# Four of twenty-two inner tiles of each feed-forward leave the seven-product scheme on their way out

## The chip, the cores and the metric

The kernel runs on one core of a Trainium2 chip. TensorE (PE) multiplies, VectorE (DVE), ScalarE (ACT) and GpSimd (POOL) do the elementwise work, SyncE (SP) issues the DMAs. Each engine works through its own queue in order, and semaphores tie the queues together. The metric is the device time of one launch in microseconds, the median of repeated runs; beside it stands one profiled launch, from which every row below is taken.

## The reference

One block of a decoder: a feed-forward, a token mixer (pooling and a gated delta rule), and a second feed-forward, each behind an RMS norm with shift and scale and a gate from a conditioning vector. Only the two feed-forwards are touched by the change:

```python
def swiglu(h, w_in, w_out):
    gate, up = jnp.split(h @ w_in, 2, axis=-1)
    return (jax.nn.silu(gate) * up) @ w_out

x = x + 0.5 * gate[:, 0, None, :] * swiglu(h, ffn1_w_in[l], ffn1_w_out[l])
```

There are 1024 tokens, the model width is 1024 and the hidden width 2816, which is 22 inner tiles of 128. All is float32.

## The kernel before

**Data.** Activations lie with the model dimension on partitions: `x[k][hf]` is 128 rows of the width by one half (512) of the tokens, k from 0 to 7, hf 0 or 1. A float32 operand is split into a high part, which ACT casts to the type fp32r (L134), and a low part, which DVE subtracts (L135). A product of two split operands takes three matmuls of 128x128 by 512. Weights come by DMA into `raw` (seven buffers), and their split halves go to `whi`/`wlo` (a ring of three pairs in the feed-forwards).

**In.** For an inner tile f, `both` forms gate and up for both halves of the tokens. It does so by a seven-product scheme of the Strassen-Winograd kind: seven `product` calls of 12 matmuls (L440, 84 in all), with DVE sums of weights and of PSUM banks between them, and a `yield` behind each product. At its end `gated_tile` (L457) multiplies silu(gate) by up and leaves the two halves as plain float32 tiles `gf`. The pool "g" has N_G = 10 buffers.

**Out.** Tiles 0 and 1 go plainly: `sweep` runs them through `middle` (plain products), splits the results (`gated`), and `out` calls `accumulate` (L297 to L304): for each 128 rows of the output six matmuls and one DVE update of x (L303). Tiles 2 to 21 go in five groups of four through `out_group`: seven products n = 1, 6, 7, 2, 4, 5, 3, each over two pairs of tiles (p = 0, 1), 12 matmuls a piece, 168 a group, a `yield` behind each of the 14 steps. Each step splits a weight and a tile (`oph`/`opl`); n = 6, 2 and 5 also form sums and differences (eight a pair, sixteen a group); when p = 1, DVE updates x from the banks (L555), 32 updates a group.

**Order.** `ffn` weaves them: while the `both` steps of a group run, every second one is followed by one step of the group before. So the 28 steps in of one group carry the 14 steps out of the group before. Behind the last group nothing is left to weave with: its 14 steps run alone, with their sums on POOL (`eng=G`, lines L371, L525, L538) in place of DVE. x of half 0 is complete when n = 4 has been added; at n = 5 `done(0)` begins what follows for half 0, while the 48 matmuls of n = 5 and 3 still run for half 1. In the first feed-forward `done(0)` is the norm in front of the mixer (`squares`, `rstd_rows`, `norm_steps`: L230 to L273); in the second it is the final norm and the store (`finish`, L751 to L771). The framework's planner lays down each engine's queue from the order in which the code emits the instructions and from its own forecast of when each is ready.

PSUM has eight banks; out products use `PSUM_OUT = ("inv", "inv", "scan", "oo")`, in products `pj` and `t`, two each.

Of the kernel before, what the change touches and what calls it, by code (L numbers as in the profile page):

```python
# [13 lines left out]
ALU = mybir.AluOpType  # L14
AX = mybir.AxisListType

P = 128
# [3 lines left out]
HALF = 512  # L21
# [45 lines left out]
def block(tc, ctx, xT, vec, cst, invw, ada_w, f1_in, f1_out, f2_in, f2_out, mix_in, mix_ba,  # L67
# [229 lines left out]
    def accumulate(x, gs, ws, gate, hf, mh, steps):  # L297

        for m in range(NC):
# [4 lines left out]
                                   in1=x[k][hf], op0=ALU.mult, op1=ALU.add)  # L304
            next(steps, None)

    def sweep(n, ins, outs, middle, x, gate, done=None, lead=None, between=iter(())):


        for j in range(0, n, 2):  # L310
            js = (j, j + 1)
            last = j == n - 2
            g = {}

            def middles(pairs):
                w = {}
                for i, hf in pairs:
                    if i not in w:
                        w[i] = ins(i)
                    g[i, hf] = middle(i, hf, w[i])  # L320

            def out(hfs, steps=iter(())):
                for mh in range(NH):
                    ws = [outs(i, mh) for i in js]
                    for hf in hfs:
                        accumulate(x, [g[i, hf] for i in js], ws, gate, hf, mh, steps)
                for _ in steps:
                    pass

            if lead:  # L330
                out(range(NH), lead(js, middles, g))
            elif last:
                steps = None
                for hf in range(NH):
                    middles([(i, hf) for i in js])
                    out([hf], steps or iter(()))
                    steps = done(hf)
            else:
                middles([(i, hf) for i in js for hf in range(NH)] if j else
                        [(i, hf) for hf in range(NH) for i in js])  # L340
                out(range(NH), islice(between, 5 * NC))
# [7 lines left out]
    def ffn(fpool, x, h, w_in, w_out, gate, done, between=(), first=None):  # L349
# [20 lines left out]
        def sub(out, a, b, eng=V):  # L370
            eng.tensor_tensor(out=out, in0=a, in1=b, op=ALU.subtract)  # L371
# [75 lines left out]
            for k in range(4):  # L447
                terms(ps, w, hs[k], k, start and k == 0, k == 3, not start)

        def both(f, out):  # L450

            (a11, a12), (a21, a22) = [[load(w_in[f, :, i, c * HALF:(c + 1) * HALF])
                                       for c in range(2)] for i in range(2)]
            h11, h21, h22 = h[0][:4], h[0][4:], h[1][4:]
            s1, s2 = nt[:, 0, :], nt[:, 1, :]

            def gated_tile(a, b):  # L457
                t = fpool.tile([P, HALF], F32, tag="g", name="gf", bufs=N_G)
                V.tensor_tensor(out=t, in0=a, in1=b, op=ALU.mult)
                out.append(t)  # L460

            c11, c12 = bank("pj"), bank("t")
            product(c11, a11, h11)
            yield
            u = act()
            S.copy(u, c11)
            V.tensor_tensor(out=s1, in0=a21, in1=a22, op=ALU.add)
            product(c12, s1, sums["1"])
            yield
            v = act()  # L470
            S.copy(v, c12)
            sub(s2, s1, a11)
            product(c11, a12, h21, start=False)
            yield
            g0 = act()
            S.activation(g0, c11, AF.Silu)
            p6 = bank("pj")
            product(p6, s2, sums["2"])
            yield
            V.tensor_tensor(out=u, in0=u, in1=p6, op=ALU.add)  # L480
            sub(s2, a12, s2)
            product(c12, s2, h22, start=False)
            yield
            g1 = act()
            V.tensor_tensor(out=g1, in0=u, in1=c12, op=ALU.add)
            S.activation(g1, g1, AF.Silu)
            p7 = bank("t")
            sub(s1, a11, a21)
            product(p7, s1, sums["3"])
            yield  # L490
            V.tensor_tensor(out=u, in0=u, in1=p7, op=ALU.add)
            V.tensor_tensor(out=v, in0=u, in1=v, op=ALU.add)
            p4 = bank("pj")
            product(p4, a22, sums["4"])
            yield
            V.tensor_tensor(out=u, in0=u, in1=p4, op=ALU.subtract)
            gated_tile(g0, u)
            gated_tile(g1, v)

        def out_group(fs, gs, eng=V, half_done=None):  # L500


            def w(f, mh):
                return load(w_out[f * P:(f + 1) * P, mh * HALF:(mh + 1) * HALF])

            def s_tile():
                return fpool.tile([P, HALF], F32, tag="s", name="s", bufs=2)

            ab = [(fs[i], fs[i + 1], gs[fs[i]], gs[fs[i + 1]]) for i in range(0, GROUP, 2)]
            s2, s3 = {}, {}  # L510
            banks, steps = None, iter(())
            for n in (1, 6, 7, 2, 4, 5, 3):
                if n in (1, 2, 4, 5):
                    banks = [bank(tag) for tag in PSUM_OUT]
                chained = n in (6, 7, 3)
                if n == 5 and half_done:
                    steps = half_done()
                for p, (f0, f1, (b11, b12), (b21, b22)) in enumerate(ab):

                    if n == 1:  # L520
                        a, b = w(f0, 0), b11
                    elif n == 6:
                        a11, a21, a22 = w(f0, 0), w(f0, 1), w(f1, 1)
                        sub(b12, b22, b12, eng)
                        eng.tensor_tensor(out=b11, in0=b11, in1=b12, op=ALU.add)  # L525
                        s2[p], s3[p] = s_tile(), a11
                        sub(a11, a11, a21, eng)
                        sub(s2[p], a22, a11, eng)
                        a, b = s2[p], b11
                    elif n == 7:  # L530
                        a, b = s3[p], b12
                    elif n == 2:
                        a, b = w(f1, 0), b21
                    elif n == 4:
                        a, b = w(f1, 1), b21
                    elif n == 5:
                        a, a22, b = w(f0, 1), w(f1, 1), b11
                        eng.tensor_tensor(out=a, in0=a, in1=a22, op=ALU.add)  # L538
                    else:
                        a, b = s2[p], b22  # L540
                    ah, op = pair(), tuple(fpool.tile([P, HALF], F32R, tag="op" + e, name="op" + e,
                                                      bufs=N_OP) for e in "hl")
                    split(a, *ah)
                    split(b, *op)
                    if n == 2:
                        sub(s2[p], a, s2[p], eng)
                        sub(b21, b21, b11, eng)
                        sub(b11, b22, b11, eng)
                    for m in range(NC):
                        terms(banks[m], ah, op, m, p == 0 and not chained, p == 1, chained)  # L550
                        if p == 1:
                            for mh, hf in {1: [(0, 0)], 6: [(0, 1)], 7: [(1, 0), (1, 1)], 2: [(0, 0)],
                                           4: [(1, 0)], 5: [(1, 1)], 3: [(0, 1)]}[n]:
                                k = mh * NC + m
                                V.scalar_tensor_tensor(out=x[k][hf], in0=banks[m],  # L555
                                                       scalar=mod[:, gate, k:k + 1], in1=x[k][hf],
                                                       op0=ALU.mult, op1=ALU.add)
                        next(steps, None)
                    yield
            for _ in steps:  # L560
                pass

        pools = ExitStack()
        steps = chain(h_sums(), between)
        sweep(2, lambda f: [weight(w_in[f, :, i, :], D) for i in range(2)],
              lambda f, mh: weight(w_out[f * P:(f + 1) * P, mh * HALF:(mh + 1) * HALF], HALF)[0],
              middle, x, gate, lead=lead)
        outs = iter(())
        for f0 in range(2, FT, GROUP):
            fs = list(range(f0, f0 + GROUP))  # L570
            gs = {f: [] for f in fs}
            for i, _ in enumerate(chain(*(both(f, gs[f]) for f in fs))):
                next(steps, None)
                if i % 2:
                    next(outs, None)
            last = f0 + GROUP == FT
            outs = out_group(fs, gs, G if last else V, (lambda: done(0)) if last else None)
        for _ in steps:
            pass
        for _ in outs:  # L580
            pass
        done(1)
        pools.close()

# [834 lines left out]
```

## Time and profile before

| what | value |
|---|---|
| median of 3 runs | 2564.01 us (2563.77 to 2565.46) |
| profiled launch, its own time | 2562.3 us |
| span of its instructions | 2560.5 us |
| mean granted TensorE clock, as a share | 0.982 |
| PE busy / weight loads busy / DVE / ACT / POOL | 96% / 79% / 76% / 39% / 10% |

The first feed-forward ends near 750 us, the mixer runs from there, and the second feed-forward fills the end from near 1890 us. A matmul's listed time (0.39 us) is longer than the distance between two starts, because matmuls overlap; so PE's pace is read from starts, or from counts in a window.

### The profile page before, as it was taken

Reading aid. Unit: us, or ns where it says so; the run is one execution under the profiler, and the core shown is the slowest. Engines: PE = TensorE matmul, PEld = TensorE weight load, DVE = VectorE, ACT = ScalarE, POOL = GpSimd, SP = SyncE. Lnnn points to the kernel's source line nnn. Section 1 sums busy time; section 2 is a strip of 40 time slices with the busy share of each in tenths; the row PEclk is TensorE's granted clock in tenths of the full one; section 3 lists DMA queues with packets and bytes.
Section 4 is the critical chain, followed back from the end, with each engine's and each line's share of the span. In section 5 each row is a group of like instructions: output and inputs, shape, how many; then the busy total and the mean of one; then the engine's idle time right before and its main releaser. Section 6 shows DMA issues by size and latency. Waiting matters only on the chain. (4 is left out here: it accounts for less than half of the span.)

```text
span 2560.5 us, 33699 instructions
## 1 busy us (share of the span) xinstructions
PE 2460.6 (96%) x12472; PEld 2015.4 (79%) x12472; DVE 1954.1 (76%) x3320; ACT 1010.8 (39%) x1710; POOL 267.1 (10%) x266
## 2 busy tenths in 40 slices
PE   5899999999979999999999999999999999999996
PEld 5678888888757888888888888788777888888874
DVE  5998978888767867767778853677678687888887
ACT  3433333333345544454454542311453333333333
POOL 2400000000240001012000000000250000000024
PEclk9999999999989999999999999999999999999997
DMA  7334422222221121121111122754321222222221
GB/s 231 110 114 125 140 79 73 69 67 80 95 107 55 34 66 64 47 72 62 47 46 46 38 88 91 250 190 152 91 66 50 64 82 69 70 70 66 80 88 68
DMA packets 122710, 224.21 MB, mean 88 GB/s; under 512 B 13744, under 2 KB 14512, under 8 KB 122544
## 3 DMA queue, kind: packets, MB, share of 16 engines
q1 hardware_dynamic: 122544, 222.04, 27.1%
q8 instruction: 98, 1.61, 0.2%
q14 instruction: 68, 0.56, 0.1%
HBM read 196.82 MB, written 25.17 MB: 87 GB/s over the span
## 5 line engine op out<-in xcount | busy, mean ns | idle before, releaser
L134 ACT CAST whi<-raw 128x512 fp32r<-128x512 f32 (+1 forms) x403 | 247.9, 617 | 608.3 <-PE ps_pj L165 157.4
L135 DVE TENSOR_TENSOR wlo<-raw,whi 128x512 fp32r<-128x512 f32 (+1 forms) x403 | 287.5, 717 | 87.2 <-ACT whi L134 85.6
L165 PE MATMUL ps_pj<-hh,whi 128*128 128x512 f32 (+1 forms) x732 | 304.6, 416 | 4.2 <-ACT whi L134 4.2
L165 PE MATMUL ps_pj<-hl,whi 128*128 128x512 f32 (+1 forms) x732 | 289.7, 396 | 0.0
L165 PE MATMUL ps_pj<-hh,wlo 128*128 128x512 f32 (+1 forms) x732 | 289.7, 396 | 0.0
L134 ACT CAST whi<-nt 128x512 fp32r<-128x512 f32 x160 | 99.3, 621 | 238.2 <-PE ps_pj L440 131.9
L165 PEld LDWEIGHTS ps_pj<-hh,whi 128*128 128x128 f32 (+1 forms) x732 | 137.6, 188 | 28.8 <-ACT whi L134 4.6
L165 PEld LDWEIGHTS ps_pj<-hh,wlo 128*128 128x128 f32 (+1 forms) x732 | 137.1, 187 | 28.8 <-issue 0.2
L165 PEld LDWEIGHTS ps_pj<-hl,whi 128*128 128x128 f32 (+1 forms) x732 | 137.8, 188 | 23.0 <-issue 1.2
L135 DVE TENSOR_TENSOR wlo<-nt,whi 128x512 fp32r<-128x512 f32 x160 | 112.0, 701 | 50.9 <-ACT whi L134 50.0
L440 PE MATMUL ps_pj<-hh,wlo 128*128 128x512 f32 x320 | 124.8, 390 | 1.0 <-DVE wlo L135 1.0
L440 PE MATMUL ps_pj<-hh,whi 128*128 128x512 f32 x320 | 124.9, 390 | 0.0
L440 PE MATMUL ps_pj<-hl,whi 128*128 128x512 f32 x320 | 124.8, 390 | 0.0
L371 POOL TENSOR_TENSOR gf<-gf 128x512 f32<-128x512 f32 x12 | 20.9, 1746 | 991.5 <-ACT whi L134 965.1
L440 PE MATMUL ps_inv<-opl,whi 128*128 128x512 f32 x280 | 113.2, 404 | 4.9 <-DVE opl L135 4.4
L440 PE MATMUL ps_inv<-oph,whi 128*128 128x512 f32 x280 | 110.5, 398 | 5.7 <-DVE x L555 4.4
L555 DVE SCALAR_TENSOR_TENSOR x<-ps_inv,mod,x 128x512 f32<-128x512 f32 x160 | 111.7, 743 | 2.7 <-PE ps_inv L440 2.5
L440 PE MATMUL ps_inv<-oph,wlo 128*128 128x512 f32 x280 | 111.3, 398 | 0.0
L135 DVE TENSOR_TENSOR opl<-gf,oph 128x512 fp32r<-128x512 f32 x140 | 103.0, 739 | 6.6 <-ACT oph L134 6.2
L862 DVE SCALAR_TENSOR_TENSOR cacc<-rawseq,vt,cacc 128x512 f32<-128x512 f32 x144 | 107.3, 746 | 0.6
L165 PE MATMUL ps_pj<-hxh,whi 128*128 128x512 f32 (+1 forms) x252 | 103.3, 411 | 0.0
L134 ACT CAST oph<-gf 128x512 fp32r<-128x512 f32 x140 | 86.3, 616 | 36.5 <-PE ps_oo L440 26.6
(465 smaller groups left out, 6404.1 us busy)
## 6 DMA issues: line engine op xcount, KB each, us to landing
raw<-f_in SPq DMA_DIRECT2D x184, 256.0 KB, 3.4
raw<-f_out SPq DMA_DIRECT2D x168, 256.0 KB, 2.8
raw<-ada_w SPq DMA_DIRECT2D x112, 256.0 KB, 3.1
raw<-mix_in SPq DMA_DIRECT2D x104, 256.0 KB, 2.8
ada_raw<-ada_w SPq DMA_DIRECT2D x32, 256.0 KB, 3.7
sg_dram<-sg SPq DMA_DIRECT2D x32, 256.0 KB, 2.0
act<-sg_dram SPq DMA_DIRECT2D x32, 256.0 KB, 4.1
raw<-dn_proj SPq DMA_DIRECT2D x20, 256.0 KB, 2.9
```

Source lines behind the costliest of these rows:

```text
L134: S.copy(hi, src)
L135: lo_eng.tensor_tensor(out=lo, in0=src, in1=hi.bitcast(F32), op=ALU.subtract)
L165: PE.matmul(ps, lhsT=a, rhs=b, start=n == 0, stop=n == last)
L371: eng.tensor_tensor(out=out, in0=a, in1=b, op=ALU.subtract)
L440: PE.matmul(ps, lhsT=u[:, c * P:(c + 1) * P], rhs=v, start=start and n == 0, stop=stop and n == 2, skip_group_check=chained)
L555: V.scalar_tensor_tensor(out=x[k][hf], in0=banks[m], scalar=mod[:, gate, k:k + 1], in1=x[k][hf], op0=ALU.mult, op1=ALU.add)
L862: V.scalar_tensor_tensor(out=acc, in0=raw[:, i:i + HALF], scalar=w[:, i:i + 1], in1=acc, op0=ALU.mult, op1=ALU.add)
```

## The change

Tiles 2 and 3 are formed by `both` as before, but leave as split pairs (`pairs=True`), and a new function `out_pair` runs them plainly through `accumulate`, half 1 first. Four groups of four (tiles 4 to 19) stay. Tiles 20 and 21 are formed by `both` as split pairs too; one step of the last group follows every one of their 14 steps (`each=1`). Then `out_pair` runs tiles 20 and 21 plainly, first half 0 alone, then half 1 alone with the steps of `done(0)` between its products; the weights are loaded and split for each of the two calls. `out_group` loses its engine choice (all its sums are on DVE) and its call of `done(0)`.

```diff
+    def out_pair(outs, js, g, hfs, x, gate, steps=iter(())):
+        for mh in range(NH):
+            ws = [outs(i, mh) for i in js]
+            for hf in hfs:
+                accumulate(x, [g[i, hf] for i in js], ws, gate, hf, mh, steps)
+        for _ in steps:
+            pass
...
             def gated_tile(a, b):
+                if pairs:
+                    V.tensor_tensor(out=a, in0=a, in1=b, op=ALU.mult)
+                    out.append(gated(fpool, a))
+                    return
...
-        def out_group(fs, gs, eng=V, half_done=None):
+        def out_group(fs, gs):
...
-                if n == 5 and half_done:
-                    steps = half_done()
...
+        def tiles_of(fs, outs, each, pairs=False):
+            gs = {f: [] for f in fs}
+            for i, _ in enumerate(chain(*(both(f, gs[f], pairs) for f in fs))):
+                next(steps, None)
+                if i % each == each - 1:
+                    next(outs, None)
+            for _ in outs:
+                pass
+            return {(f, hf): gs[f][hf] for f in fs for hf in range(NH)} if pairs else gs
+
         outs = iter(())
-        for f0 in range(2, FT, GROUP):
+        js = (2, 3)
+        out_pair(pair_out, js, tiles_of(js, outs, 2, True), (1, 0), x, gate)
+        for f0 in range(4, FT - 2, GROUP):
             fs = list(range(f0, f0 + GROUP))
-            gs = {f: [] for f in fs}
-            for i, _ in enumerate(chain(*(both(f, gs[f]) for f in fs))):
-                next(steps, None)
-                if i % 2:
-                    next(outs, None)
-            last = f0 + GROUP == FT
-            outs = out_group(fs, gs, G if last else V, (lambda: done(0)) if last else None)
+            outs = out_group(fs, tiles_of(fs, outs, 2))
+        js = (FT - 2, FT - 1)
+        g = tiles_of(js, outs, 1, True)
         for _ in steps:
             pass
-        for _ in outs:
-            pass
+        out_pair(pair_out, js, g, [0], x, gate)
+        out_pair(pair_out, js, g, [1], x, gate, done(0))
         done(1)
```

## Rows read from the trace of the kernel before

**Rows 1.** The page: busy time, then PE's busy tenths in 40 slices.

```profile
PE 2460.6 (96%) x12472; PEld 2015.4 (79%) x12472; DVE 1954.1 (76%) x3320; ACT 1010.8 (39%) x1710; POOL 267.1 (10%) x266
PE   5899999999979999999999999999999999999996
```

**Rows 2.** Busy by window, second feed-forward: two tiles unwoven, then one woven group.

```profile
core 0: us, PE busy (x) PEld busy (x) DVE busy (x) ACT busy (x) POOL busy (x), PEclk, DMA share, GB/s
1982.00:2020.70 38.70, 38.70 (x169) 31.55 (x168) 25.18 (x40) 13.54 (x23) 0.00 (x0) 1.00 0.19 57
...
2251.70:2367.20 115.50, 115.50 (x506) 94.62 (x505) 93.81 (x150) 41.80 (x72) 0.00 (x0) 1.00 0.24 73
```

**Rows 3.** First feed-forward's end in order of time: start, length, what.

```profile
689.46 0.62 PE L440 MATMUL ps_inv<-oph,whi 128*128 128x512 f32 x2
...
724.64 0.39 PE L440 MATMUL ps_oo<-oph,wlo 128*128 128x512 f32 x1
...
725.53 0.74 DVE L555 SCALAR_TENSOR_TENSOR x<-ps_oo,mod,x 128x512 f32<-128x512 f32 x1
...
749.41 0.40 PE L440 MATMUL ps_oo<-oph,wlo 128*128 128x512 f32 x1
...
753.97 0.69 PE L165 MATMUL ps_pj<-hh,whi 128*64 128x512 f32 x1 [4.16 <-ACT whi L134]
```

**Rows 4.** Second feed-forward's end in order of time.

```profile
2483.49 0.62 PE L440 MATMUL ps_inv<-oph,whi 128*128 128x512 f32 x2
...
2518.95 0.39 PE L440 MATMUL ps_oo<-oph,wlo 128*128 128x512 f32 x1
...
2519.38 0.75 DVE L555 SCALAR_TENSOR_TENSOR x<-ps_oo,mod,x 128x512 f32<-128x512 f32 x1
...
2537.41 0.39 PE L440 MATMUL ps_oo<-oph,wlo 128*128 128x512 f32 x1
...
2545.72 0.69 DVE L230 TENSOR_TENSOR act<-act,nt 128x512 f32<-128x512 f32 x1
...
2551.78 5.36 DVE L770 SCALAR_TENSOR_TENSOR x<-x,vt,ps_pj 128x512 f32<-128x512 f32 x8 [3.25 <-PE ps_pj L175]
```

**Rows 5.** What PE waited for, 688.7 to 770 us: total, times, longest.

```profile
PE ps_scan L440 <- DVE x L555: 2.6, 5, 1.3
PE ps_oo L440 <- DVE x L555: 2.4, 5, 1.1
```

**Rows 6.** Plain out products at the mixer's end, in order of time.

```profile
1721.05 0.39 PE L165 MATMUL ps_inv<-gh,whi 128*128 128x512 f32 x1
...
1721.73 0.39 PE L165 MATMUL ps_inv<-gh,whi 128*128 128x512 f32 x1
```

**Rows 7.** DVE's two commonest forms in 2251.7 to 2367.2 us: busy, mean ns.

```profile
L135 DVE TENSOR_TENSOR wlo<-raw,whi 128x512 fp32r<-128x512 f32 x22 | 15.1, 687 | 4.1 <-ACT whi L134 3.9
...
L555 DVE SCALAR_TENSOR_TENSOR x<-ps_inv,mod,x 128x512 f32<-128x512 f32 x16 | 11.1, 743 | 0.0
```

**Rows 8.** The page's DMA issues: the weights of the way out.

```profile
raw<-f_out SPq DMA_DIRECT2D x168, 256.0 KB, 2.8
```

**Rows 9.** PE in `sweep` of tiles 0 and 1, second feed-forward, weight change.

```profile
1929.23 0.50 PE L165 MATMUL ps_inv<-gh,whi 128*128 128x512 f32 x1 [0.92 <-DVE x L303]
1931.09 0.50 PE L165 MATMUL ps_inv<-gh,wlo 128*128 128x512 f32 x1 [1.13 <-DVE wlo L135]
```

**Rows 10.** The norm of half 0 and the mixer's first weights, first feed-forward.

```profile
735.98 2.72 DVE L268 SCALAR_TENSOR_TENSOR nt<-x,coef,ps_pj 128x512 f32<-128x512 f32 x4 [0.74 <-PE ps_pj L175]
...
740.85 9.18 POOL L135 TENSOR_TENSOR hl<-nt,hh 128x512 fp32r<-128x512 f32 x7 [0.45 <-ACT hh L134]
...
753.31 2.17 ACT L134 CAST whi<-raw 128x512 fp32r<-128x512 f32 x4
```

**Rows 11.** `finish` of half 0, and the sums of squares of half 1.

```profile
2527.12 1.06 PE L247 MATMUL ps_t<-ct,act 128*128 128x1 f32 x8
...
2531.39 11.75 POOL L768 TENSOR_TENSOR x<-x,act 128x512 f32<-128x512 f32 x8 [1.91 <-ACT act L762]
...
2538.65 6.24 DVE L230 TENSOR_TENSOR act<-act,nt 128x512 f32<-128x512 f32 x5
```

More of the change, by code (lines that the diff above doesn't have):

```diff
@@ L322, in out @@
             def out(hfs, steps=iter(())):
[L323 to L327, printed above, removed]
-                    pass
+                out_pair(outs, js, g, hfs, x, gate, steps)
             if lead:
@@ L448, in product, with both @@
                 terms(ps, w, hs[k], k, start and k == 0, k == 3, not start)
-        def both(f, out):
+        def both(f, out, pairs=False):
             (a11, a12), (a21, a22) = [[load(w_in[f, :, i, c * HALF:(c + 1) * HALF])
@@ L510, in out_group @@
             s2, s3 = {}, {}
-            banks, steps = None, iter(())
+            banks = None
             for n in (1, 6, 7, 2, 4, 5, 3):
@@ L523, in out_group @@
                         a11, a21, a22 = w(f0, 0), w(f0, 1), w(f1, 1)
-                        sub(b12, b22, b12, eng)
-                        eng.tensor_tensor(out=b11, in0=b11, in1=b12, op=ALU.add)
+                        sub(b12, b22, b12)
+                        V.tensor_tensor(out=b11, in0=b11, in1=b12, op=ALU.add)
                         s2[p], s3[p] = s_tile(), a11
-                        sub(a11, a11, a21, eng)
-                        sub(s2[p], a22, a11, eng)
+                        sub(a11, a11, a21)
+                        sub(s2[p], a22, a11)
                         a, b = s2[p], b11
@@ L537, in out_group @@
                         a, a22, b = w(f0, 1), w(f1, 1), b11
-                        eng.tensor_tensor(out=a, in0=a, in1=a22, op=ALU.add)
+                        V.tensor_tensor(out=a, in0=a, in1=a22, op=ALU.add)
                     else:
@@ L545, in out_group @@
                     if n == 2:
-                        sub(s2[p], a, s2[p], eng)
-                        sub(b21, b21, b11, eng)
-                        sub(b11, b22, b11, eng)
+                        sub(s2[p], a, s2[p])
+                        sub(b21, b21, b11)
+                        sub(b11, b22, b11)
                     for m in range(NC):
@@ L557, in out_group, with pair_out @@
                                                        op0=ALU.mult, op1=ALU.add)
-                        next(steps, None)
                     yield
-            for _ in steps:
-                pass
         pools = ExitStack()
         steps = chain(h_sums(), between)
+        def pair_out(f, mh):
+            return weight(w_out[f * P:(f + 1) * P, mh * HALF:(mh + 1) * HALF], HALF)[0]
         sweep(2, lambda f: [weight(w_in[f, :, i, :], D) for i in range(2)],
-              lambda f, mh: weight(w_out[f * P:(f + 1) * P, mh * HALF:(mh + 1) * HALF], HALF)[0],
-              middle, x, gate, lead=lead)
+              pair_out, middle, x, gate, lead=lead)
+        def tiles_of(fs, outs, each, pairs=False):
[7 more added lines that the diff above has]
+            return {(f, hf): gs[f][hf] for f in fs for hf in range(NH)} if pairs else gs
         outs = iter(())
-        for f0 in range(2, FT, GROUP):
+        js = (2, 3)
+        out_pair(pair_out, js, tiles_of(js, outs, 2, True), (1, 0), x, gate)
+        for f0 in range(4, FT - 2, GROUP):
             fs = list(range(f0, f0 + GROUP))
-            gs = {f: [] for f in fs}
-            for i, _ in enumerate(chain(*(both(f, gs[f]) for f in fs))):
-                next(steps, None)
-                if i % 2:
-                    next(outs, None)
-            last = f0 + GROUP == FT
-            outs = out_group(fs, gs, G if last else V, (lambda: done(0)) if last else None)
+            outs = out_group(fs, tiles_of(fs, outs, 2))
+        js = (FT - 2, FT - 1)
+        g = tiles_of(js, outs, 1, True)
         for _ in steps:
             pass
-        for _ in outs:
-            pass
+        out_pair(pair_out, js, g, [0], x, gate)
+        out_pair(pair_out, js, g, [1], x, gate, done(0))
         done(1)
```

## The prediction, as put down before the changed kernel ran

> **What bounds the kernel now.** The page comes first: PE is busy 96% of the span, and its slices show nine tenths or more almost everywhere [rows 1]. So a gain has to come from the few places where PE waits, and every matmul added costs its full time. Next the windows of the woven stretch: in a group's period of 115.5 us PE is busy throughout, and the period holds 4 x 84 + 168 = 504 matmuls, so one takes 115.5 / 504 = 0.229 us. DVE is busy 93.8 us of it, 81%, and keeps up [rows 2]. Plain out products start three matmuls apart by 0.68 us, 0.227 us each [rows 6].
>
> Then the two ends in order of time. The last group runs unwoven. In the first feed-forward its 120 matmuls up to n = 4 last from 689.5 to 725.0, 35.5 us where 120 x 0.229 = 27.5 would do; the 48 of n = 5 and 3 last until 749.8, 24.8 where 11.0 would do [rows 3]. In the second it is 2483.5 to 2519.3 (35.8) and on to 2537.8 (18.5) [rows 4]. PE stands idle 8.0 + 13.8 and 8.3 + 7.5 us there. The list of PE's waits names DVE's updates of x first [rows 5]: banks come back late, because an unwoven product has nothing else to give PE meanwhile. Behind the first end the mixer's first matmul starts at 754.0, released by ACT's cast of a weight [rows 3]; behind the second lie 22.7 us from the last matmul to the end of the span, 2560.5.
>
> **The change, part by part.**
>
> *Matmuls.* Per feed-forward a group of 168 goes and two plain pairs of 96 come, 24 more. In time: 192 x 0.227 = 43.6 us in place of 168 x 0.229 = 38.5, so 5.1 us more. This is sure, and falls twice.
>
> *The stretch of one to one.* Tiles 20 and 21 give 168 matmuls, the group beside them 168: 336 x 0.229 = 77.0 us of PE. DVE there: a tile unwoven takes 25.18 / 2 = 12.6 us; a group 93.8 - 4 x 12.6 = 43.4 [rows 2]; the four splits of the pairs 4 x 0.687 = 2.7 [rows 7]. Sum 2 x 12.6 + 43.4 + 2.7 = 71.3 us, 93% where 81% has been shown to be covered. No row shows PE beside a DVE so full. From below the stall is 0: 71.3 is under 77. From above it is the unwoven group's own rate, 8.3 us over 120 matmuls, so 11.6 over 168. The demand is uneven: n = 6, 7 and 2 carry most of the sums and a double update. With every DVE operation at its full 0.69 or 0.74 us [rows 7], 84 x 0.69 + 32 x 0.74 = 81.6, which is 4.6 over. I take 2 us, nearer to the woven row, because the two products of a step come from independent chains and DVE is below full in the sum. Tile 20 wants four "g" buffers when six steps of the group have run: two of ten are free and n = 7 has given back two, so this fits with nothing over.
>
> *Plain pairs.* The ring holds three pairs of weights, and a pair of products keeps two until its last matmul; the next second weight is then split late. In the existing plain sweep one such change cost 0.92 + 1.13 us [rows 9]. The new code has one for tiles 2 and 3 and three for tiles 20 and 21, each 0 to 2 us. I take 1 us for the first pair with its hand-over and 2.4 for the second, half of it before half 0 is done. Loads of `f_out` fall from 168 to 2 x (4 + 64 + 4 + 8) = 160 of 256 KB [rows 8]; that is no term. Splits and updates in a plain pair are light on DVE (8 splits and 16 updates, 17 us against 21.8 of matmuls), so what DVE owes after the woven stretch is paid here.
>
> *Sum, second feed-forward.* Matmuls: 2483.5 + 43.6 = 2527.1; stalls 2 + 1 + 2.4; and 2 us for the small matmuls of `finish(0)`, which PE takes in order between those of half 1 (8 take 1.06 us, and the broadcast waits for POOL) [rows 11]. The last big matmul ends at 2534.5 in place of 2537.8: 3.3 us gained. Behind it: before, half 1 ended with rows k = 0 to 3, so all seven sums of squares came after the last update, from 2538.65 to 2546.4 [rows 4, 11]. Now k = 4 to 7 come last, and the sums of 2 and 3, and some of 4 to 6, run under the matmuls. I leave 3.5 of them, at 6.24 / 5 = 1.25 us, as they run beside POOL, so 4.4 us in place of 7.8: 3.4 gained. POOL's scaling of half 0 does not get in front: its sum starts 2.7 us after half 0's last update (2522.4), and from the first small matmul to the end of the scaling it is 2543.14 - 2527.12 = 16.0 us [rows 11], so POOL is free at 2541.1, about when `finish(1)` needs it. Together 6.7 us.
>
> *Sum, first feed-forward.* Half 0's last update: 689.5 + 144 x 0.227 = 722.2, one update and its wait 1.0, stalls 2 + 1 + 1.2, so 727.4; before 726.3 [rows 3]. From there to the mixer's first matmul it was 27.7 us: 9.7 to the first scaled row (735.98), 14.0 until POOL has written the last low part (750.0), then squares of half 1, then the weight's cast at 753.3 [rows 10]. Now DVE has fewer splits and no differences of n = 3 in between: I take 8 to the first row and 13 for the norm, where POOL needs 9.18 / 7 = 1.31 us a row. If ACT casts weights only behind all that, the sum is some 25; if it casts them as soon as the last plain products free the ring, 13 us after half 0, the sum is 14.5. I take 22, nearer to the order that the rows show. The mixer starts at 749.4 in place of 754.0: 4.6 gained.
>
> Both: 6.7 + 4.6 = 11.3 us, from 2562.3 to 2551.0 in the profiled launch. The median of the runs lies 1.7 above that launch, so 2552.7; I say 2553.
>
> *A rule against it.* In `finish` DVE's adds took 1.25 us beside POOL's scaling, and 0.69 alone [rows 4, 11]; the change moves more of them under that scaling. The Trainium skill, SBUF — State Buffer, section Who interferes with whom, says that DVE instructions with two SBUF inputs and GpSimd's reads exclude each other for a whole instruction. By it an add could wait out a whole POOL operation, 11.75 / 8 = 1.47 us, and take 2.16; 3.5 of them would cost 7.6 in place of 4.4, and the sum would be 2556. The trace's 1.25 is nearer to half a wait, and I keep it.
>
> **The rivals.** One part in five hundred, 5 us, is about what a measurement of this kernel can tell from no change.
>
> *More is won.* The woven stretch does not stall (2 us less for each feed-forward), and ACT casts the mixer's weights early: half 0 at 725.4, the mixer at 739.9, 14.1 gained; the second end 8.7. Together 22.8: 2541. For it speaks that the raw weights lie ready; against it that ACT was without a gap in the norm before.
>
> *Nothing changes.* The mixer starts on the same chain (25 us), and the stretch of one to one stalls 4.5 us: half 0 at 729.9, the mixer at 754.9, 0.9 lost; the second end gains 4.2. Together 3 gained: 2561. For it speaks that ACT, not PE, released the mixer's first matmul [rows 3].
>
> *Slower: DVE becomes the bound beside the last group.* DVE's queue is in order; a sum of n = 6 or 2 that stands ahead of a split makes PE wait, and the update that frees a bank stands behind both. If the stretch keeps the unwoven group's rate, 11.6 us in place of 2, the cost is 9.6 for each, 19.2, and 11.3 - 19.2 = 7.9 lost: 2572. It decides from a stall of 2 + 5.6 = 7.6 us for each. For it speaks DVE's 93%; against it that in the woven stretch no wait of PE is left at 81%.
>
> **How the numbers follow.** Forecast 0.50 (its own range 2546 to 2560, by 0 to 2 us a weight change, 0 to 4.6 for the woven stall and 20 to 24 us to the mixer), more 0.15, nothing 0.17, slower 0.18. The forecast leaves 0.02 of itself within 5 us of no change. Faster 0.63, same 0.19, slower 0.18. The range takes in the gain at 2541 and half of the slower case: 2540 to 2568.
>
> **What would show it.** In the profile after: no unwoven group before the plain pair, and PE above 95% busy in the 77 us in front of it, with DVE above 90%; PE's waits there under 5 us. Plain pairs of 21.8 us with one short wait at a change of weights. POOL without L371, L525 and L538 at the ends. Half 0's last update about 1 us later than before in the first feed-forward, and the mixer's first matmul about 5 us earlier; from the last big matmul to the end some 19.5 us in place of 22.7. The prediction is wrong if PE waits for DVE's splits or updates over 7 us beside the last group, if each change of weights costs over 2 us, or if the mixer starts on ACT's chain at 754 or later.

## The result: 2542.2 us, 0.9% faster, with the profile after

The changed kernel ran in 2542.19 us (median, 2540.96 to 2543.36), the kernel before beside it in 2564.07 (2563.77 to 2565.46). The ratio is 0.9914, 95% interval 0.9896 to 0.9931: 21.9 us gained, where 11 were forecast. The profiled launch took 2543.36 us, its span is 2541.5 in place of 2560.5; the 19.0 us between the two spans are what the traces can explain.

The page of the kernel after, against [rows 1] and [rows 8]:

```profile
PE 2458.6 (97%) x12520; PEld 2019.6 (79%) x12520; DVE 1937.8 (76%) x3304; ACT 1003.2 (39%) x1694; POOL 218.0 (9%) x234
PE   5899999999999999999999999899999999999997
...
raw<-f_out SPq DMA_DIRECT2D x160, 256.0 KB, 2.8
```

PE executes 48 matmuls more, 24 for each feed-forward, and the dip in the twelfth slice, the first feed-forward's end, is gone.

Windows of the kernel after (columns as in [rows 2]): nearly the whole of both stretches of one to one, the last plain pair of the second feed-forward, and what follows it.

```profile
636.70:715.00 78.30, 77.46 (x334) 62.30 (x334) 68.70 (x111) 31.44 (x54) 0.17 (x3) 1.00 0.30 91
2417.30:2495.70 78.40, 77.55 (x335) 62.37 (x334) 68.77 (x110) 29.22 (x50) 0.00 (x0) 1.00 0.26 81
...
2495.70:2520.00 24.30, 22.98 (x107) 18.27 (x106) 22.16 (x32) 16.90 (x30) 10.28 (x7) 1.00 0.06 22
...
2520.30:2541.50 21.20, 3.94 (x16) 3.56 (x16) 12.50 (x16) 1.32 (x3) 9.25 (x6) 0.56 0.45 173
```

Beside the last group PE is busy 99% of the stretch at a granted clock of 1.00 (2.4 GHz), with DVE at 88%. From tile 20's first matmul to the first one of the plain pair, the two stretches last from 634.71 to 713.69 and from 2415.41 to 2494.40:

```profile
634.71 0.39 PE L444 MATMUL ps_pj<-hh,whi 128*128 128x512 f32 x1
...
2415.41 0.39 PE L444 MATMUL ps_pj<-hh,whi 128*128 128x512 f32 x1
...
2494.40 0.39 PE L165 MATMUL ps_inv<-gh,whi 128*128 128x512 f32 x1
```

That is 79.0 us for 336 matmuls in either, 2.0 us more than their 77.0. The waits of PE from 636 to 760 us name L444, the line of the group's products and of `both`'s, three times, with 0.8 us in all; two of the three:

```profile
PE ps_pj L444 <- DVE wlo L135: 0.3, 1, 0.3
PE ps_oo L444 <- DVE x L560: 0.2, 1, 0.2
```

The first feed-forward's end after, in order of time, against [rows 3] and [rows 10]:

```profile
713.69 0.39 PE L165 MATMUL ps_inv<-gh,whi 128*128 128x512 f32 x1
...
725.60 0.74 DVE L303 SCALAR_TENSOR_TENSOR x<-ps_oo,mod,x 128x512 f32<-128x512 f32 x1
...
732.35 0.62 ACT L134 CAST whi<-raw 128x512 fp32r<-128x512 f32 x1 [0.50 <-ACT act L234]
734.00 2.72 DVE L268 SCALAR_TENSOR_TENSOR nt<-x,coef,ps_pj 128x512 f32<-128x512 f32 x4 [0.71 <-PE ps_pj L175]
...
737.99 9.63 POOL L135 TENSOR_TENSOR hl<-nt,hh 128x512 fp32r<-128x512 f32 x7 [0.46 <-ACT hh L134]
...
739.63 0.39 PE L165 MATMUL ps_oo<-gh,wlo 128*128 128x512 f32 x1
739.85 0.40 PE L165 MATMUL ps_pj<-hh,whi 128*64 128x512 f32 x1
...
742.05 0.50 PE L165 MATMUL ps_t<-hh,whi 128*128 128x512 f32 x1 [1.58 <-ACT whi L134]
...
744.84 0.69 PE L165 MATMUL ps_pj<-hh,wlo 128*64 128x512 f32 x1 [2.06 <-DVE wlo L135]
```

The mixer's first matmul (739.85) stands one matmul's pitch behind the last plain one (739.63): PE goes from the one to the other without a wait. Before, it came at 753.97, released by ACT. ACT casts a weight at 732.35, before the norm's first scaled row (734.00) is there. Two waits, of 1.58 and 2.06 us, come right behind.

The end of the second after, against [rows 4] and [rows 11]:

```profile
2506.32 0.73 DVE L303 SCALAR_TENSOR_TENSOR x<-ps_oo,mod,x 128x512 f32<-128x512 f32 x1
...
2515.49 13.05 POOL L782 TENSOR_TENSOR x<-x,act 128x512 f32<-128x512 f32 x8 [1.91 <-ACT act L776]
...
2519.87 0.39 PE L165 MATMUL ps_oo<-gh,wlo 128*128 128x512 f32 x1
...
2522.33 0.74 DVE L303 SCALAR_TENSOR_TENSOR x<-ps_oo,mod,x 128x512 f32<-128x512 f32 x1
2522.99 1.09 DVE L230 TENSOR_TENSOR act<-act,nt 128x512 f32<-128x512 f32 x1
2524.12 1.63 DVE L230 TENSOR_TENSOR act<-act 128x512 f32<-128x512 f32 x1
2525.86 1.57 DVE L230 TENSOR_TENSOR act<-act,nt 128x512 f32<-128x512 f32 x1
...
2527.48 1.86 PE L247 MATMUL ps_t<-ct,act 128*128 128x1 f32 x8 [7.22 <-DVE act L230]
```

The last update ends 2.8 us behind the last big matmul (2523.07 against 2520.26; before, 0.8), because adds of 1.09 us stand between the updates. From the last big matmul to the end of the span it is 21.2 us in place of 22.7.

**Where the 19.0 us are.** The second feed-forward starts its plain matmuls at 1902.1 in place of 1913.4: 11.3 us come from the first feed-forward's end. Taken from there, the last big matmul is 6.2 us earlier (2537.80 - 2520.26 - 11.3), and 1.5 come behind it: 7.7.

**What the stall of the kernel before was made of.** First, where the unwoven group begins:

```profile
686.74 0.39 PE L440 MATMUL ps_inv<-oph,whi 128*128 128x512 f32 x1
...
687.40 0.74 DVE L555 SCALAR_TENSOR_TENSOR x<-ps_oo,mod,x 128x512 f32<-128x512 f32 x1
...
692.17 1.40 DVE L555 SCALAR_TENSOR_TENSOR x<-ps_inv,mod,x 128x512 f32<-128x512 f32 x2
...
2480.77 0.39 PE L440 MATMUL ps_inv<-oph,whi 128*128 128x512 f32 x1
```

The update at 687.40 is the last one of the group before, whose last step ends in front of 686.74. The next updates, from 692.17 on, belong to the step that starts at 689.46 [rows 3]; so that step is p = 1 of n = 1, and the 12 matmuls from 686.74 on are p = 0. The last group therefore begins at 686.74, and at 2480.77 in the second feed-forward, one step ahead of where the prediction begins it. Its 120 matmuls up to n = 4 last 38.1 and 38.4 us where 120 x 0.227 = 27.3 would do. The stall is 10.8 and 11.1 us, not 8.0 and 8.3.

Windows of the kernel before, the group from its second step on, up to and behind its n = 4:

```profile
689.46:724.64 35.18, 30.07 (x109) 20.97 (x107) 29.85 (x42) 12.78 (x23) 19.01 (x11) 0.95 0.29 98
724.64:749.81 25.17, 19.49 (x66) 13.17 (x64) 18.88 (x28) 15.44 (x28) 14.32 (x11) 0.80 0.26 100
2483.49:2518.95 35.46, 30.58 (x108) 21.48 (x107) 30.63 (x42) 15.09 (x27) 17.60 (x11) 0.90 0.07 23
2518.95:2537.80 18.85, 15.85 (x66) 11.69 (x64) 14.98 (x20) 10.10 (x18) 10.32 (x8) 0.91 0.11 43
```

The mean granted clock is 0.80 to 0.95 in them, so PE was at its lower level, 1.2 GHz, part of the time. Single matmuls of the kernel before show it, just behind four waits for updates of x:

```profile
2505.19 0.80 PE L440 MATMUL ps_oo<-oph,whi 128*128 128x512 f32 x1 [0.52 <-DVE x L555]
...
2506.81 0.63 PE L440 MATMUL ps_inv<-opl,whi 128*128 128x512 f32 x1
2507.23 0.63 PE L440 MATMUL ps_inv<-oph,wlo 128*128 128x512 f32 x1
...
2510.72 0.39 PE L440 MATMUL ps_inv<-opl,whi 128*128 128x512 f32 x1
```

Here they start 0.42 us apart, and 0.23 again from 2510.7 on. The prediction called the whole loss "idle"; part of it was matmuls at the low level. An estimate from the starts of the matmuls up to n = 4: of the 10.8 and 11.1 us, 9.1 and 8.7 lie in single gaps of over 0.5 us between two starts, most of them behind a wait for an update of x, and 1.6 and 2.4 in runs of matmuls 0.3 to 0.5 us apart. The Trainium skill, TensorE: Matmul & The Clock Gate, section A second HAM failure mode: psum-queue depth-cycling, describes a kernel whose clock goes back and forth because PE pauses briefly between groups of matmuls while it cycles through PSUM banks. This trace agrees: waits of 0.5 to 0.8 us for banks, then 2505 to 2510 at the low level; after the change the stretch of one to one has a clock of 1.00.

### The profile page after: what moved, and what is told of

The parts are those of the page before. It is cut to its first block, busy times and chain, and to the rows that moved or that the text cites. A ratio compares the mean times of both kernels' runs of the same rounds, so it can differ in the third digit from the quotient of the medians.

```text
span 2541.5 us, 33684 instructions
## 1 busy us (share of the span) xinstructions
PE 2458.6 (97%) x12520; PEld 2019.6 (79%) x12520; DVE 1937.8 (76%) x3304; ACT 1003.2 (39%) x1694; POOL 218.0 (9%) x234
## 3 DMA queue, kind: packets, MB, share of 16 engines
q1 hardware_dynamic: 121392, 219.95, 27.3%
## 5 line engine op out<-in xcount | busy, mean ns | idle before, releaser
L134 ACT CAST whi<-raw 128x512 fp32r<-128x512 f32 x407 | 250.6, 618 | 608.3 <-PE ps_pj L165 162.1
L135 DVE TENSOR_TENSOR wlo<-raw,whi 128x512 fp32r<-128x512 f32 x407 | 290.6, 718 | 76.8 <-ACT whi L134 74.8
L165 PEld LDWEIGHTS ps_pj<-hh,whi 128*128 128x128 f32 (+1 forms) x732 | 137.6, 188 | 24.2 <-issue 2.9
L165 PEld LDWEIGHTS ps_pj<-hl,whi 128*128 128x128 f32 (+1 forms) x732 | 137.9, 188 | 23.1 <-issue 1.4
L444 PE MATMUL ps_pj<-hh,wlo 128*128 128x512 f32 x320 | 125.0, 391 | 1.7 <-DVE wlo L135 1.7
L444 PE MATMUL ps_pj<-hh,whi 128*128 128x512 f32 x320 | 125.1, 391 | 0.5 <-ACT whi L134 0.5
L444 PE MATMUL ps_pj<-hl,whi 128*128 128x512 f32 x320 | 124.8, 390 | 0.0
L165 PE MATMUL ps_pj<-hxh,wlo 128*128 128x512 f32 (+1 forms) x252 | 99.2, 394 | 0.0
L165 PE MATMUL ps_pj<-hxl,whi 128*128 128x512 f32 (+1 forms) x252 | 98.8, 393 | 0.0
L230 POOL TENSOR_TENSOR act<-act,nt 128x512 f32<-128x512 f32 x18 | 26.5, 1470 | 815.7 <-ACT nt L237 815.3
L560 DVE SCALAR_TENSOR_TENSOR x<-ps_inv,mod,x 128x512 f32<-128x512 f32 x128 | 89.3, 744 | 0.2
L444 PE MATMUL ps_inv<-opl,whi 128*128 128x512 f32 x224 | 87.7, 392 | 0.0
L444 PE MATMUL ps_inv<-oph,whi 128*128 128x512 f32 x224 | 87.3, 391 | 0.0
L444 PE MATMUL ps_inv<-oph,wlo 128*128 128x512 f32 x224 | 86.8, 389 | 0.0
```

The lines of the kernel that those rows point to most:

```text
L134: S.copy(hi, src)
L135: lo_eng.tensor_tensor(out=lo, in0=src, in1=hi.bitcast(F32), op=ALU.subtract)
L165: PE.matmul(ps, lhsT=a, rhs=b, start=n == 0, stop=n == last)
L230: eng.tensor_tensor(out=a, in0=a, in1=b, op=ALU.add)
L444: PE.matmul(ps, lhsT=u[:, c * P:(c + 1) * P], rhs=v, start=start and n == 0, stop=stop and n == 2, skip_group_check=chained)
L560: V.scalar_tensor_tensor(out=x[k][hf], in0=banks[m], scalar=mod[:, gate, k:k + 1], in1=x[k][hf], op0=ALU.mult, op1=ALU.add)
```

## The experiments

The kernel before had medians of 2564.0 to 2565.0 us beside them; the kernel after is 2542.2 (ratio 0.9914).

**1. The old order, sums on DVE.** The last group's operand sums go from POOL to DVE, everything else as before.

```diff
-            outs = out_group(fs, gs, G if last else V, (lambda: done(0)) if last else None)
+            outs = out_group(fs, gs, V, (lambda: done(0)) if last else None)
```

> The kernel before, with the sums of the last group of four on VectorE in place of GpSimd; nothing else changed. Theory W (the gain comes from giving the last group company and from the plain end): the group is still unwoven, 16 operations of 0.6 to 0.7 us move to VectorE in each feed-forward and VectorE's operations no longer wait for GpSimd; these about cancel, so 2558 to 2570 us. Rival P (the gain comes from taking the sums off GpSimd, whose operations of 1.3 to 2.3 us stood in front of splits): most of the 22 us come already here, 2542 to 2552 us.

Measured: 2555.01 us, ratio 0.9964 (0.9951 to 0.9976), 9.8 us faster than before; it lies between the two expectations. The group got no shorter: its last big matmul starts at 752.4 in the first feed-forward, where [rows 3] has 749.4, and PE waits for DVE's splits instead. Waits of PE (688 to 770 us), one line of the timeline, and two of the second end:

```profile
PE ps_inv L440 <- DVE opl L135: 4.7, 3, 3.3
```

```profile
2522.38 11.10 POOL L768 TENSOR_TENSOR x<-x,act 128x512 f32<-128x512 f32 x8 [2.68 <-ACT act L762]
...
2532.65 3.91 DVE L230 TENSOR_TENSOR act<-act,nt 128x512 f32<-128x512 f32 x5
```

The gain lies behind the group. POOL scales half 0 from 2522.4 on in place of 2531.4, so five adds of half 1 take 3.91 us in place of 6.24 [rows 11]; from the last big matmul's start to the end of the span it is 20.8 us in place of 23.1. In the mixer the first convolution comes at 784.8 in place of 789.7. ACT casts a weight of the mixer in the middle of half 1's squares, and the mixer's first matmul (752.60) stands right behind the last one of the group (752.37):

```profile
748.24 0.60 ACT L134 CAST whi<-raw 128x512 fp32r<-128x512 f32 x1
```

So some 10 us were to be had without weaving; they are not a share of the 21.9 that adds to the others (see 5).

**2. The group unwoven again.** The last group runs out before tiles 20 and 21; the plain pairs stay.

```diff
         g = tiles_of(js, outs, 1, True)
...
+        for _ in outs:
+            pass
         js = (FT - 2, FT - 1)
```

> The changed kernel, with the 14 steps of the last group of four written out before tiles 20 and 21 begin, so that the code weaves them with nothing. Theory W: the unwoven stall comes back, 8 to 12 us in each feed-forward less what the planner interleaves by itself: 2552 to 2566 us. Rival P: the sums are on VectorE as before, so 2540 to 2545 us.

Measured: 2558.5 us, 0.9975 (0.9966 to 0.9983): 16.3 slower than after. The last big matmul of the first feed-forward is 7.6 us later (747.2), the second feed-forward 9.5 longer from its first plain matmul to its last. From its first matmul (633.41) to tile 20's first product (682.57) the group takes 49.2 us, where its 168 matmuls and the two of tile 20 that stand among them would take 38.6. Timeline of the unwoven group, and its window:

```profile
654.02 0.50 PE L444 MATMUL ps_scan<-oph,whi 128*128 128x512 f32 x1 [0.81 <-DVE x L560]
655.34 0.50 PE L444 MATMUL ps_oo<-oph,whi 128*128 128x512 f32 x1 [0.81 <-DVE x L560]
```

```profile
633.41:682.57 49.16, 44.17 (x172) 32.37 (x170) 46.46 (x75) 15.57 (x28) 0.00 (x0) 0.97 0.20 59
```

The same waits for double updates return, and a clock of 0.97, with all sums on DVE and nothing of a norm beside them. The stall is 10.6 us, near the 10.8 that the kernel before lost up to n = 4; woven it is 2.0. The weave is what takes it away.

**3. Both halves together in the last plain pair.**

```diff
-        out_pair(pair_out, js, g, [0], x, gate)
-        out_pair(pair_out, js, g, [1], x, gate, done(0))
+        out_pair(pair_out, js, g, (0, 1), x, gate)
+        for _ in done(0):
+            pass
```

> The changed kernel, with the last plain pair in one call for both halves (weights loaded once) and what follows for half 0 begun behind it. If the cover of the last 48 matmuls matters (W): half 0 is complete 24 matmuls, 5.4 us, later; the mixer starts some 5 us later and the end of the kernel 0 to 4 us later, 2546 to 2552 us. If what follows half 0 has slack (rival): 2539 to 2544 us.

Measured: 2549.83 us, 0.9941 (0.9928 to 0.9955): 7.6 slower than after. The plain pair itself ends earlier (736.6 against 739.6: no second set of weights, no small matmuls between), but the norm of half 0 then lies bare: the mixer's matmuls start 7.5 us behind the last plain one (744.0), the second feed-forward 5.1 us later, and at the end of the kernel 30.8 us pass from the last big matmul's start in place of 21.6. These rows come from a launch of 2553.7 us, 3.9 above the median. So one half after the other, with half 0's norm under half 1, is worth 7.6 us.

**4. Two more pairs plain.** Tiles 4 to 7 go as two plain pairs, so one group of seven products fewer.

```diff
-        js = (2, 3)
-        out_pair(pair_out, js, tiles_of(js, outs, 2, True), (1, 0), x, gate)
-        for f0 in range(4, FT - 2, GROUP):
+        for js in ((2, 3), (4, 5), (6, 7)):
+            out_pair(pair_out, js, tiles_of(js, outs, 2, True), (1, 0), x, gate)
+        for f0 in range(8, FT - 2, GROUP):
```

> The changed kernel, with tiles 4 to 7 also run plainly as two pairs and three groups of four left; 24 matmuls more in each feed-forward. By the price of the forecast (5.1 us for 24 matmuls, and about 0.7 us for each change of weights): 2 x (5.1 + 1 to 2) = 12 to 14 us slower than the changed kernel, 2554 to 2557 us. If a plain pair costs only its matmuls: 2552. If matmuls added there were covered (rival: PE is not the bound in the first part): 2542 to 2546 us.

Measured: 2560.44 us, 0.9983 (0.9974 to 0.9992): 18.2 slower than after, above the 12 to 14 expected. The last group's last matmul is 10.6 us later in the first feed-forward and 7.5 in the second, of which 24 x 0.227 = 5.5 are the matmuls. The rest is in part small waits: those for ACT's casts of g grow from 0.7 to 1.9 us in the first and from 1.4 to 2.8 in the second, those for updates of x in plain products from 0.5 to 1.4 in the first, and some 1 to 3 us stay unassigned. So exchanging one more group for two pairs costs 7.5 to 10.6 us. What the change's own exchange cost isn't measured by itself; the ends more than pay for it.

**5. The woven group's sums on POOL.** As before the change, but in the woven form.

```diff
-                        sub(a11, a11, a21)
-                        sub(s2[p], a22, a11)
+                        sub(a11, a11, a21, eng)
+                        sub(s2[p], a22, a11, eng)
...
-            outs = out_group(fs, tiles_of(fs, outs, 2))
+            outs = out_group(fs, tiles_of(fs, outs, 2), G if f0 + GROUP == FT - 2 else V)
```

> The changed kernel, with the sums of the woven last group on GpSimd in place of VectorE. Theory W (VectorE at 93% beside the last group is enough, PE is the bound there): no change within 3 us, 2539 to 2546 us; where VectorE was late, up to 2 us faster. Rival P (sums on GpSimd hold up what PE needs): 8 to 16 us of the gain go, 2550 to 2558 us.

Measured: 2541.75 us, 0.9908 (0.9895 to 0.9922): no difference from after. What cost 9.8 us in the old order (1) costs nothing here. The two orders differ in the weave and in the norm beside the group; no run tells which of the two makes the engine of the sums matter, though in 1 the gain lies at the norm, behind the group.

**6. The mixer's ring in another order.** The mixer's split weights take the five new buffers first, then the feed-forward's three.

```diff
-        wring.set((wpool, 3), (rows, 5))
+        wring.set((rows, 5), (wpool, 3))
```

> The changed kernel, with the mixer's ring of split weights begun by the five buffers of its own pool in place of the three that the feed-forward used. Theory R (the mixer starts 14 us earlier because ScalarE can cast its first weights as soon as the last plain products free the ring, ahead of the rest of the norm): the own pool lies where the feed-forward's tiles lay, which are free later, so the first weights are cast later; the mixer's first matmul moves from 13.5 us behind half 0 to 17 to 25, 2545 to 2554 us. Rival: the norm of half 0 alone sets the mixer's start, and the time stays at 2540 to 2544 us.

Measured: 2549.14 us, 0.9936 (0.9922 to 0.9949): 7.0 slower than after, as one theory said, but not in its way. The mixer's first matmul starts at 740.04, as in the kernel after, since the first cast stays where it was (732.49). Another product comes first, and PE waits behind it for the low part of its weight, then again for the norm:

```profile
744.99 0.79 PE L165 MATMUL ps_inv<-hh,wlo 128*128 128x512 f32 x1 [4.32 <-DVE wlo L135]
...
754.61 1.05 PE L247 MATMUL ps_oo<-ct,act 128*128 128x1 f32 x8 [2.35 <-DVE act L230]
```

So this doesn't test whether the early cast lets the mixer start early. It shows that the order of products which this ring brings costs 7 us, and that the time of the first matmul alone says little.

**7. Sums of squares as columns on PE.** In the final norm of half 1 the last squares are no longer added by DVE; PE sums three sets of columns and DVE reduces them.

```diff
+        accs = acc if isinstance(acc, list) else [acc]
+        for i, a in enumerate(accs):
+            for c in range(NC):
+                PE.matmul(ps[:, i * NC + c:i * NC + c + 1], lhsT=a[:, c * P:(c + 1) * P],
+                          rhs=ones[:, 0:1], start=True, stop=True)
...
-            total = squares(x, hf, engs=(G, V) if hf == 0 else (V, V))
...
```

> The changed kernel, with the last sum of squares of half 1 in the final norm taken by PE: the two partial sums and the square of row 7 go to PE as three sets of columns, and VectorE adds 128x4 numbers. If VectorE's adds beside GpSimd's scaling set the end (they take 1.1 to 1.6 us each): two adds of 1.6 us leave the chain and one small reduction enters, 2 to 3 us faster, 2539 to 2540 us. If GpSimd's scaling of half 0 is next in line (it ends 1 us before the final power needs it): 1 us or nothing, 2541 to 2543 us.

Measured: 2542.89 us, 0.9918 (0.9905 to 0.9932): nothing gained. Two adds are gone, but PE's 24 small matmuls run at the low clock there (0.50 from 2521.7 to 2527) and take their place:

```profile
2521.68 3.58 PE L249 MATMUL ps_t<-ct,act 128*128 128x1 f32 x16 [3.88 <-DVE act L785]
2525.11 1.84 PE L249 MATMUL ps_t<-ct,nt 128*128 128x1 f32 x8
```

**8. Half 0's scaling left out.**

```diff
-                    G.tensor_tensor(out=t, in0=t, in1=rs, op=ALU.mult)
+                    pass
```

> POOL's product with the reciprocal root is left out of the final norm of half 0: its rows go out scaled by the gain alone, by ACT. It measures what POOL's eight products cost the sums of half 1 beside them. In the profile after, DVE's last four adds took 1.09, 1.09, 1.63 and 1.57 us there, against 0.69 alone. Contention theory: without POOL's products those four take 0.69 to 0.78, the way from the last update to the first small matmul of half 1 is 4.4 - 1.7 = about 2.5 us, and the whole is 2 to 3.5 us shorter than the kernel after. Rival, the adds wait for ACT's squares or the chain through PE and POOL sets the end: the adds stay where they are and the whole is within 1 us of the kernel after.

Measured: 2538.29 us, 0.9894 (0.9876 to 0.9913): 3.9 faster than after; the two kernels' times don't overlap (2536.8 to 2539.5, 2541.0 to 2543.4). The end of the second feed-forward:

```profile
2518.55 0.68 DVE L230 TENSOR_TENSOR act<-act,nt 128x512 f32<-128x512 f32 x1
2519.15 0.74 DVE L303 SCALAR_TENSOR_TENSOR x<-ps_oo,mod,x 128x512 f32<-128x512 f32 x1
2519.81 0.68 DVE L230 TENSOR_TENSOR act<-act,nt 128x512 f32<-128x512 f32 x1
2520.52 0.69 DVE L230 TENSOR_TENSOR act<-act 128x512 f32<-128x512 f32 x1
2521.32 0.69 DVE L230 TENSOR_TENSOR act<-act,nt 128x512 f32<-128x512 f32 x1
```

Without POOL every add takes 0.68 or 0.69 us. The last update ends 0.9 us behind the last big matmul in place of 2.8, the adds 2.1 behind that in place of 4.4, and from the last big matmul's start 17.5 us pass to the end of the span in place of 21.6. The updates, with one input in PSUM, take 0.74 with POOL beside them and without. The Trainium skill, SBUF — State Buffer, section Who interferes with whom, says that a DVE instruction contends with POOL's reads when two of its inputs lie in SBUF, and not with one; by that rule the adds wait and the updates don't, and the trace agrees. The size, 1.09 to 1.63 us beside products of 1.63, is less than a whole POOL operation on top of each add.

**9. Half 0's sum of squares on DVE alone.**

```diff
-            total = squares(x, hf, engs=(G, V) if hf == 0 else (V, V))
+            total = squares(x, hf, engs=(V, V))
```

> The sum of squares of half 0 goes to DVE alone, where POOL did half of it. Contention theory: POOL's three adds of 1.3 to 1.8 us go, the broadcast of half 0 and POOL's scaling begin some 2 us earlier (2513 to 2514 in place of 2515.5), so 1 or 2 of DVE's last adds of half 1 come free of POOL: 0.5 to 1.5 us shorter than the kernel after. Rival, DVE is the limit in the last plain pair (22.2 of 24.3 us busy): three more adds there delay the updates of half 1 and the whole is 0 to 2 us longer.

Measured: 2542.26 us, 0.9912 (0.9896 to 0.9928): as after. POOL's scaling starts at 2512.6, 0.9 us earlier against the last big matmul, but still lasts until 2525.4, over nearly all of the last adds, which take 1.09 to 1.63 us as before.

**10. The scaling split between POOL and DVE.** Rows 4 to 7 of half 0 go to DVE, written behind half 1's sum.

```diff
+            rows_ = [(k, 0) for k in range(4)] if hf == 0 else \
+                [(k, 0) for k in range(4, KD)] + [(k, 1) for k in range(KD)]
+            for k, hf in rows_:
...
+                if hf == 0 and k >= 4:
+                    V.scalar_tensor_tensor(out=t, in0=t, scalar=g, in1=held[0], op0=ALU.mult, op1=ALU.mult)
```

> The scaling of half 0 is split: rows 0 to 3 stay with POOL, rows 4 to 7 go to DVE, in the 3.25 us in which it waits for half 1's reciprocal root. Leaving POOL's scaling out altogether cost 4.1 us less from the last big matmul to the end (17.5 in place of 21.6). Contention theory: POOL ends at about 2522, so the last three adds take 0.7 us each; four rows on DVE take 4 x 0.67 = 2.7 us and fit the gap: 2 to 3.5 us shorter than the kernel after, as in the run without scaling less 0 to 1. Rival, the four rows and their stores come too late (they stand ahead of half 1's rows on DVE, and 12 stores of 256 KB then end together): 0 to 1 us shorter, or longer.

Measured: 2540.93 us, 0.9910 (0.9897 to 0.9924): 1.3 faster than after by the medians, within what can be told from no change. The last adds are down to 0.67 and 0.68 us, but the planner put DVE's four rows among them, not into the gap behind:

```profile
2524.50 0.74 DVE L786 SCALAR_TENSOR_TENSOR x<-x,vt,act 128x512 f32<-128x512 f32 x1
2525.16 0.68 DVE L230 TENSOR_TENSOR act<-act 128x512 f32<-128x512 f32 x1
2525.76 0.74 DVE L786 SCALAR_TENSOR_TENSOR x<-x,vt,act 128x512 f32<-128x512 f32 x1
```

What the contention gave back the rows took. With the rows held back it could win up to the 3.9 us of experiment 8; that wasn't tried.

## Why the prediction was right in direction and too low by half

The direction and the mechanism held: two plain pairs cost their 24 matmuls, the stall of the unwoven group goes, and half 1 covers half 0's norm. The steps, by the traces:

| Step | Predicted | Measured |
| --- | --- | --- |
| start of the last group before, from which both sums count | 689.46; 2483.49 | 686.74; 2480.77 |
| stall of one to one | 2 us | 2.0 in both (79.0 us against 77.0) |
| first plain pair with its hand-over, over its matmuls | 1 us | 2.4 in the first, 1.0 in the second (24.2 and 22.8 us against 21.8) |
| half 0's last update, first feed-forward | 727.4 | 726.3 |
| from there to the first scaled row; to the mixer's first matmul | 8; 22 us | 7.7; 13.5 us |
| first feed-forward's gain | 4.6 | 14.1 at the mixer's start, 11.3 kept |
| last plain pair, second feed-forward, over its matmuls | 2.4 + 2 us | 4.1 us (25.86 against 21.8) |
| last big matmul, second feed-forward, relative | 3.3 earlier | 6.2 earlier |
| behind it | 3.4 | 1.5 |
| sum in the profiled launch | 11.3 | 19.0 |

**The term that was mis-sized** is "I take 22, nearer to the order that the rows show", the way from half 0's last update to the mixer's first matmul. It measured 13.5, below the lower end of 14.5 that the prediction worked out and put aside. The start is no longer set by a chain through ACT: half 1's plain products last 13.3 us from half 0's last update (726.34 to 739.63), and PE takes the mixer's first product right behind them. Of the 9.6 us by which the mixer starts earlier than forecast, 8.5 are this term and 1.1 lie ahead of it. That the old order of ACT's queue (casts behind the squares of half 1) isn't forced shows in experiment 1, where a cast stands between these squares after a change of engine alone; that covering the norm is what counts, in experiment 3. Why ACT's first cast moved ahead of the norm's rows is read from the trace and was not tested, since experiment 6 left it in place. And 2.8 of the 14.1 us are paid back behind the start: PE's waits there sum to 3.7 us (1.58 and 2.06) where they were 1.8 before, and the rest isn't assigned.

**Twelve matmuls were counted twice.** Both sums take the matmuls behind 689.46 and 2483.49 as a whole group and put 192 new ones in their place. But the group's first step, 12 matmuls or 2.7 us, lies in front of these times. So each sum ends 2.7 us too late. In the first feed-forward this hid stalls 1.6 us larger than booked, and half 0 came out 1.1 us early. In the second the stalls were as forecast, 2.0 + 1.0 + 4.1 against 2 + 1 + 4.4, and the 2.9 us more that the last big matmul gained are this slip almost alone. The stall of the unwoven group was misread by the same 2.7 us.

**The tail** gained 1.5 in place of 3.4: the adds behind the last update cost 4.4 us, as forecast, but the adds ahead of it, at 1.09 instead of 0.69, made the last update itself 2 us late. The sum counted the contention only where it was at the end of the chain; experiment 8 puts all of it at 4.1 us.

**The rivals.** "DVE becomes the bound" needed a stall of 7.6 us; it was 2.0 in both, with DVE at 88%, below the 93% worked out. Experiment 2 shows that DVE's updates do hold PE up when nothing is woven beside them; with a second chain of products PE stayed 99% busy beside a DVE at 88%. "Nothing changes" fell with the mixer's start. "More is won" named the outcome: its 2541 came from the mixer at 739.9 (measured 739.85) and no stall. The early cast was right, but the stretch did stall 2.0 us, the 12 matmuls counted twice hid it, and 2.8 us were paid back later; that the number fits so well is in part luck.

The medians differ by 21.9 and the profiled spans by 19.0: before, the profiled launch was 1.8 us under its median, after, 1.2 over it.

**What stays open:** the parts overlap. The weave is worth 16.3, the order of the halves 7.6, the engine of the sums 9.8 in the old order and nothing in the new one, so they can't be added to 21.9. How much of the old stall was wait and how much low clock is only estimated from the trace, and only up to n = 4.

## What to carry to other kernels

Where one engine sets the pace and waits for banks in only one place, give it a second independent chain of products there, even if the exchange adds work: here 24 matmuls (5.5 us) bought off a group's stall of some 11 us up to its n = 4, low clock included. Order the last products so that one half of the data is done early and its norm runs under the other half, and let the end of that cover, not the old chain, be the forecast of what comes next. When moving work under a neighbour's, count contention for every operation ahead of the last one too, not only for those behind it.

## What was not expected of the hardware

- The granted clock fell inside a stretch in which PE was 77 to 86% busy: waits of 0.5 to 0.8 us for banks, then matmuls 0.42 us apart in place of 0.23 for 5 us. Just ahead of that PE had been busy 2.36 us from 2500 to 2505; from 2505 to 2510 the granted clock was 0.50.
- Matmuls of 128x1 depend on the clock as the large ones do: 8 took 0.94 us right behind big matmuls (experiment 3) and 1.86 after PE had waited 7.2 us, at a granted clock of 0.50 (2525 to 2530).
- Contention between DVE and POOL goes both ways: an add took 1.09 to 1.63 us in place of 0.69, and POOL's products 13.05 / 8 = 1.63 in place of 1.47 [rows 11] and of 11.10 / 8 = 1.39 (experiment 1), where fewer adds ran beside them.
